# Gate one-hots laid out by token, one gate matmul a token, and the expert selection later in the weave of a 256-token network on one core

## The chip, the cores and the metric

The kernel runs on one core of a Trainium2 chip. The metric is device time of one execution in microseconds (us). "DVE" is VectorE, "ACT" ScalarE, "PE" TensorE (its weight loads are "PEld"), "POOL" GpSimd and "SP" the engine that issues the weight DMAs. Every engine runs its own list of instructions in order.

## What is computed

One layer of four token mixers, a gated feed-forward, two attentions, and at the end product-key experts; 256 tokens, model width 1024. Only the experts matter here:

```
scores of 8 heads against two sets of 128 keys   -> the 16 best of each set, with their places
sums of pairs of those                           -> the 16 best pairs, softmax over the 16: gates
expert (i, j), i and j in 0..127 (16384 of them): act = gelu(x . eu[i, j]),  out += gate * act * ev[i, j]
```

The kernel computes all 16384 experts for all 256 tokens densely, and a matrix of gates `G[i, j, t]` (nearly all zero) multiplies the activations. `G` comes from one-hot products: for a token t with its 128 chosen triples (i, j, gate), held on the 128 partitions, `G[:, :, t] = onehot(i)^T . (onehot(j) * gate)`. The one-hots are f16; so that the gate keeps its precision it is scaled by 4096 and split into a high and a low f16 part, whose two products are summed.

## The kernel before

Weights stream in units of [128, 1024] f32 (512 KB): a DMA on SP into `raw`, a copy on ACT into `hi` (`prefetch`, recorded as L139), a subtraction `lo = raw - hi` (L157) on POOL or DVE, three buffers of each. A column tile of a product is one unit and 24 matmuls of 256 columns in `dense_n` (L301): 16 with `hi`, 8 with `lo`. For the units of `eu` the subtraction is POOL's, for those of `ev` DVE's.

The experts run in two halves of 64 (j = 0..63, then 64..127). I call the parts stage A (`experts_u` of the first half: 64 units, with the selection and the first half's gates woven in), the first `experts_v`, stage B (`experts_u` of the second half with its gates woven in) and the second `experts_v`. The selection and the gates are generators; `weave(main, side, counts)` lets `main` emit a unit and then takes `counts[i]` steps of `side`. The order in which the code runs is the order of the instructions on every engine.

- `gen_a` (stage A): 8 steps of top-16 of pairs, a step of ranks, a step of softmax (an exponential on ACT between DVE work), four steps that look up the places (`ixr` by ACT, `eq` twice and a sum into `sel` by DVE), two steps that transpose `sel` on PE and make `IT`, `JT`, `GHL`; then `open_gates` (an iota on POOL) and 33 steps of `gates3`. `CA` is its list of counts.
- `gen_b` (stage B): 33 steps of `gates3`; `CB` is its list.
- A step of `gates3` makes the one-hots of 8 tokens on DVE (`oi`, `eqj`, `jg`; two buffers each) and then issues the matmuls of the 8 tokens before them (L1739 and L1740, one with the high and one with the low gate part), and the copy of the result from PSUM into `Gt` (ACT, scaled by 1/4096). `prep(0)` ends each generator; it multiplies activations by gates and splits them for the second matmul.

PSUM banks have tags: `m` four banks (held by the output sums from stage A on), `n` two, `d` two. In stages A and B of the kernel before, units and gate steps took banks of `d` and `n` in rotation.

Of the kernel before, what the change touches and what calls it, by code (L numbers as in the profile page):

```python
# [10 lines left out]
F16 = mybir.dt.float16  # L11
I32 = mybir.dt.int32
U32 = mybir.dt.uint32
AF = mybir.ActivationFunctionType
# [10 lines left out]
# ---------------------------------------------------------------- constants of the shapes alone  # L25
# [53 lines left out]
# per-partition parameters: name -> columns  # L79
# [19 lines left out]
CA = [1, 1, 0] * 8 + [1] * 36  # L99
CB = [0] * 4 + [1, 1, 0] * 18  # L100
# [11 lines left out]
def _emit(ctx, tc, I, out):  # L112
# [8 lines left out]
    BANKS = {"m": 4, "n": 2, "d": 2}  # L121
    turn_ = {"i": 0, "d": ["d"]}

    def bank(tag="m"):
        if tag == "d":
            turn_["i"] += 1
            tag = turn_["d"][turn_["i"] % len(turn_["d"])]
        return ps.tile([128, 512], F32, tag=tag, name="b" + tag, bufs=BANKS[tag])

# [11 lines left out]
    # ------------------------------------------------------------ weights: a stream of [128,1024] units  # L141
# [43 lines left out]
    # ------------------------------------------------------------ loads  # L185
# [29 lines left out]
    def rsqrt(pool, src, n, name, scale=1.0, out=None, w=None):  # L215
        """(src * scale + eps) ** -0.5 for src [128, n]."""
# [12 lines left out]
    def gained(gain, hi, lo, acc=None):  # L229
        """xT += acc; hi, lo <- the parts of xT * gain."""  # L230
# [10 lines left out]
    def stats(pool, tag="nsq", w=256, bufs=4):  # L241
        """R <- rsqrt(mean(xT^2) + eps) of a token on all partitions, Rc with tokens on partitions."""
# [51 lines left out]
    def dense_n(name, idx, o, M=128, X=None, part=None):  # L294
        """o [M,256] <- one column tile (K = 1024) of a product with X."""
# [9 lines left out]
    def dense_2(name, idx, d, X=None, part=0, of=4):  # L305
        """a part of two column tiles of a product with X, into d [128,512]: the products with X's low parts last."""
# [15 lines left out]
    def rows_into(acc, name, ks, xs, first, last, part=None):  # L322
        """acc (4 banks, 8 column tiles of 256 tokens) += some row tiles of a product, each with its parts of xs."""
# [17 lines left out]
    def columns_into(acc, name, u, xs, first, last, part):  # L341
        """acc (2 banks, 4 column tiles of 256 tokens) += two row tiles of a product, with their parts xs."""
# [12 lines left out]
    def tokens(name, u, nk, n, banks, part=None):  # L355
        """banks [tokens, n] += the product of nk row tiles with one unit, tokens on partitions."""
# [17 lines left out]
    def follow(gens, turns):  # L374
        """the generators' steps in the order of turns, what is left of them in rotation."""
# [49 lines left out]
    # ============================================================ block 1: the four mixers  # L425
# [53 lines left out]
    # ---- projections  # L479
# [135 lines left out]
    # ---- gated delta net: decays and beta, tokens on partitions  # L615
    G4 = []

    def gdn_gates():
# [35 lines left out]
        # e^G of a token in its chunk, e^(Glast - G), e^Glast  # L654
# [15 lines left out]
    # ---- gated delta net  # L670
    def gdn():
# [14 lines left out]
        # k, v with tokens on partitions  # L686
# [20 lines left out]
        # q e^G, channels on partitions  # L707
# [8 lines left out]
        # decays of pairs inside a chunk (rows (chunk parity, token), columns (tile, head, token))  # L716
# [38 lines left out]
        # inverse of the unit lower triangles, blocks doubling  # L755
# [31 lines left out]
        # w and u, then q_in - a w and a u  # L787
# [20 lines left out]
        def tok(z, e, c):  # L808
            """[64 rows, tile, pair, 64] of a [128, pair, 256] tile, for a head parity's columns."""
# [13 lines left out]
        # the state between chunks  # L823
# [70 lines left out]
    def logsig(dst, x, n, name):  # L894
        """dst <- log sigmoid(x), both in SBUF."""
# [9 lines left out]
    def pv(o, pt0, pt1, v):  # L905
        """o [64, 256] <- the transposed output of a head; v(tile) -> [128 tokens, 64]."""
# [3 lines left out]
    # ---- attention of heads that share a bank of outputs: two steps for a head  # L910
# [55 lines left out]
    def halves(z, lv):  # L966
        """[.., 256] -> [.., groups, 2, lv]"""
# [199 lines left out]
    # ============================================================ block 1: gated feed-forward with a convolution  # L1167
# [4 lines left out]
    # rotary tables from the positions  # L1172
# [92 lines left out]
    # ============================================================ block 2: two attentions  # L1265
# [66 lines left out]
    # latent attention: projections  # L1332
    def latent(n, gain, name):
        """after the job's matmuls: its scaled rows and the sums of their squares."""
# [201 lines left out]
    def act(j):  # L1536
        """the activations of the experts j and j + 1 of a half."""
# [7 lines left out]
    # ============================================================ block 2: product-key experts  # L1545
    IT = big.tile([128, 256], F16)
    JT = big.tile([128, 256], F16)
    GHL = big.tile([128, 2, 256], F16)
# [159 lines left out]
    box = {}  # L1708
# [256 lines left out]
```

## Time and profile before

| | us |
|---|---|
| time, median of three runs | 1680.62 (1679.57 to 1684.98) |
| profiled execution, span from the first to the last instruction | 1677.0 |
| what lies between that span and the median | 3.6 |
| stage A, 807.35 to 1075.02 of the profile | 267.7 |
| stage B, 1249.11 to 1494.32 | 245.2 |

The profiled execution has no time of its own but its span. A page of the profile gives the busy time of each engine; tables of stretches split it by stage; the chain of work is followed back from the last instruction, at each step to what released it; a timeline lists single instructions with start, duration and, in brackets, how long the engine stood idle ahead of it and who ended that.

### The profile page before, as it was taken

How to read it: one execution, taken by the hardware profiler on the slowest of the kernel's cores; microseconds unless marked ns; L12 is line 12 of the kernel's file. 1: busy time of each engine (PE TensorE's matmuls, PEld its weight loads, DVE VectorE, ACT ScalarE, POOL GpSimd, SP SyncE). 2: the span in 40 equal slices, each digit the busy share in tenths (PEclk: the TensorE clock that was granted, in tenths of full speed). 3: DMA queues.
4: the chain of work that ended last, by engine and by line, in shares of the span. 5: the costliest groups of instructions: out<-in, count | busy, mean ns of one | idle time of the engine just before them, and what ended most of it. 6: DMA issues, size and time to landing. Idle time of an engine off the chain costs nothing.

```text
span 1677.0 us, 27178 instructions
## 1 busy us (share of the span) xinstructions
PE 1549.2 (92%) x11060; PEld 1416.3 (84%) x11060; DVE 1017.6 (61%) x1666; ACT 763.3 (46%) x1050; POOL 736.3 (44%) x313
## 2 busy tenths in 40 slices
PE   6799898888877999989987999999999999999997
PEld 6688677788876878879987999988889999998886
DVE  5657757888886457766995333366672222236665
ACT  5633344444443444445462444544444444554444
POOL 3543135667765445685774554300036556540000
PEclk9899878999998999999998999999999999999999
DMA  5332013444443333463543333566664444466664
GB/s 209 104 97 77 28 53 117 138 151 151 151 139 114 101 92 110 144 189 114 169 144 97 103 113 113 165 196 193 194 193 135 133 126 126 127 201 199 190 191 135
DMA packets 63791, 231.41 MB, mean 138 GB/s; under 512 B 7073, under 2 KB 7602, under 8 KB 63282
## 3 DMA queue, kind: packets, MB, share of 16 engines
q1 hardware_dynamic: 62640, 226.00, 44.0%
q10 hardware_dynamic: 1026, 3.68, 0.6%
q8 instruction: 86, 1.41, 0.4%
q14 instruction: 39, 0.32, 0.1%
HBM read 228.60 MB, written 1.05 MB: 137 GB/s over the span
## 4 chain that ended last, share of the span: by engine, by line
PE 49%; DVE 2%; ACT 0%; POOL 0%; issue 0%; DVEq 0%; ACTq 0%
PE bd L301 10%; PE bn L301 10%; PE bm L1783 7%; PE bm L1785 7%; PE bm L1784 7%; PE bn L1739 2%; PE bd L1739 2%; PE bn L1740 2%; PE bd L1740 2%; DVE eq L1680 1%; DVE eq L1678 0%; DVE eq L1676 0%; DVE sel L1681 0%; DVE oi L1725 0%; ACT fy L139 0%; DVE fz L1818 0%
## 5 line engine op out<-in xcount | busy, mean ns | idle before, releaser
L157 POOL TENSOR_TENSOR lo<-raw,hi 128x1024 fp32r<-128x1024 f32 x296 | 728.4, 2475 | 745.2 <-ACT hi L139 737.4
L139 ACT ACTIVATE hi<-raw 128x1024 fp32r<-128x1024 f32 x426 | 446.2, 1056 | 187.9 <-PE bm L1784 51.8
L301 PE MATMUL bd<-Xh,hi 128*128 128x256 f32 x1096 | 287.8, 298 | 23.7 <-ACT hi L139 15.0
L301 PE MATMUL bd<-Xl,hi 128*128 128x256 f32 x1096 | 277.4, 289 | 0.7 <-DVE Xl L238 0.7
L301 PEld LDWEIGHTS bd<-Xh,hi 128*128 128x128 f32 x1096 | 216.3, 197 | 32.0 <-ACT hi L139 17.3
L301 PEld LDWEIGHTS bd<-Xl,hi 128*128 128x128 f32 x1096 | 215.9, 197 | 1.8 <-DVE Xl L238 1.0
L157 DVE TENSOR_TENSOR lo<-raw,hi 128x1024 fp32r<-128x1024 f32 x130 | 159.2, 1226 | 95.1 <-ACT hi L139 95.1
L1783 PE MATMUL bm<-hi,eh 128*128 128x512 f32 x512 | 199.2, 389 | 0.0
L1784 PE MATMUL bm<-hi,el 128*128 128x512 f32 x512 | 199.2, 389 | 0.0
L1785 PE MATMUL bm<-lo,eh 128*128 128x512 f32 x512 | 199.2, 389 | 0.0
L1725 DVE TENSOR_TENSOR oi<-iorep,IT 128x1024 f16<-128x1024 f16 x64 | 47.2, 737 | 243.7 <-PE bn L1740 128.8
L301 PE MATMUL bn<-Xh,hi 128*128 128x256 f32 x656 | 164.2, 289 | 13.0 <-ACT hi L139 13.0
L1223 DVE SCALAR_TENSOR_TENSOR fy<-fxp,prm,fy 128x256 f32<-128x256 f32 x88 | 154.0, 1769 | 15.8 <-ACT fy L139 14.2
L301 PE MATMUL bn<-Xl,hi 128*128 128x256 f32 x656 | 160.3, 283 | 0.0
L301 PE MATMUL bd<-Xh,lo 128*128 128x256 f32 x1096 | 155.3, 285 | 2.7 <-POOL lo L157 2.6
L301 PEld LDWEIGHTS bd<-Xh,lo 128*128 128x128 f32 x1096 | 142.0, 192 | 4.5 <-POOL lo L157 4.5
L301 PEld LDWEIGHTS bn<-Xh,hi 128*128 128x128 f32 x656 | 125.4, 191 | 14.8 <-ACT hi L139 14.8
L301 PEld LDWEIGHTS bn<-Xl,hi 128*128 128x128 f32 x656 | 125.0, 191 | 0.0
L1785 PEld LDWEIGHTS bm<-lo,eh 128*128 128x128 f32 x512 | 96.1, 188 | 20.1
L1783 PEld LDWEIGHTS bm<-hi,eh 128*128 128x128 f32 x512 | 96.1, 188 | 19.8
L1784 PEld LDWEIGHTS bm<-hi,el 128*128 128x128 f32 x512 | 96.1, 188 | 19.8
L301 PE MATMUL bn<-Xh,lo 128*128 128x256 f32 x656 | 92.6, 284 | 2.6 <-POOL lo L157 2.6
(583 smaller groups left out, 2640.5 us busy)
## 6 DMA issues: line engine op xcount, KB each, us to landing
raw<-in_eu SPq DMA_DIRECT2D x128, 512.0 KB, 3.6
raw<-in_ev SPq DMA_DIRECT2D x128, 512.0 KB, 4.0
raw<-in_w_in SPq DMA_DIRECT2D x61, 512.0 KB, 3.6
raw<-in_w_up SPq DMA_DIRECT2D x44, 512.0 KB, 3.6
raw<-in_w_down SPq DMA_DIRECT2D x22, 512.0 KB, 3.6
raw<-in_w_out SPq DMA_DIRECT2D x16, 512.0 KB, 3.6
raw<-in_w_query SPq DMA_DIRECT2D x16, 512.0 KB, 3.7
raw<-in_w_ba SPq DMA_DIRECT2D x4, 512.0 KB, 3.5
```

The costliest lines, as they stand in the source:

```text
L139: S.activation(o, i, f, **kw)
L157: (V if by == "v" else G).tensor_tensor(lo[:, :width], raw[:, :width], hi[:, :width].bitcast(F32), op=OP.subtract)
L301: PE.matmul(o, w[:, k * 128:k * 128 + M], x[:, k], start=n == 0, stop=n == 23)
L1223: V.scalar_tensor_tensor(y[:, i], xp[:, i, s:s + 256], P("fcw", n * 3 + s), y[:, i], op0=OP.mult, op1=OP.add)
L1680: V.tensor_add(eq[:, :, 0:w], eq[:, :, 0:w], eq[:, :, w:2 * w])
L1725: V.tensor_tensor(oi, rep, IT[:, None, ts].to_broadcast([128, 128, 8]), op=OP.is_equal)
L1739: PE.matmul(pv_[:, t, :nj], oi[:, :, t], jg[:, 0, :nj, t], start=True, stop=False)
L1740: PE.matmul(pv_[:, t, :nj], oi[:, :, t], jg[:, 1, :nj, t], start=False, stop=True)
L1783: PE.matmul(o, eh[:, i, ts], v[0][:, n_], start=False, stop=False, skip_group_check=True)
L1784: PE.matmul(o, el[:, i, ts], v[0][:, n_], start=False, stop=False, skip_group_check=True)
L1785: PE.matmul(o, eh[:, i, ts], v[1][:, n_], start=False, stop=last and j + i == nj - 1, skip_group_check=True)
```

## The change

Four things change, all from stage A on.

1. One-hots lie token by token (`[8 tokens, 64 pairs, 2]`) and not with the 8 tokens innermost. `IT`, `JT`, `GHL` hold each value twice, so that every operand's innermost run is a pair of f16. The single multiplication into `jg` becomes two, one for each gate part.
2. One matmul of 128 columns a token streams both gate parts (8 matmuls a step and not 16), four tokens to a bank, two banks a step.
3. The two parts are summed as the result is taken out of PSUM, by `tensor_reduce` on DVE (two a step) and not a copy on ACT; the 1/4096 moves into `prep`. In the selection's lookup, four adds become one `tensor_reduce`. The transposes and gate matmuls take banks of `n`, the units those of `d`.
4. `CA` and `CB` are new. In stage A the selection's first step comes after the 15th unit of 64 and not after the first, its lookups after the 29th, 31st, 33rd and 35th, its transposes after the 37th and 38th, and the gate steps from the 39th unit on, five for four units, up to the end of the stage. In stage B there is one gate step for two units up to the 57th unit, and one after each of the last six.

```diff
-CA = [1, 1, 0] * 8 + [1] * 36
-CB = [0] * 4 + [1, 1, 0] * 18
+CA = [0] * 14 + [1] * 8 + [0, 0, 1, 0] + [1, 0] * 5 + [1, 1] + [1, 1, 2, 1] * 7
+CB = [0] * 2 + [1, 0] * 28 + [1] * 6
...
-                for w in (8, 4, 2):
-                    V.tensor_add(eq[:, :, 0:w], eq[:, :, 0:w], eq[:, :, w:2 * w])
-                V.tensor_add(sel[:, i, t].rearrange("p (h k) -> p h k", h=8), eq[:, :, 0], eq[:, :, 1])
+                V.tensor_reduce(out=sel[:, i, t].rearrange("p (h k) -> p h k", h=8),
+                                in_=eq.rearrange("p h a k -> p h k a"), op=OP.add, axis=AX.X)
...
+        def pairs(z, n):
+            return z[:, :, None, :].to_broadcast([128, 8, n, 2])
+        def along(n, j=0):
+            return row[:, None, j:j + 2 * n].to_broadcast([128, 8, 2 * n]).rearrange("p t (j e) -> p t j e", e=2)
...
-            V.tensor_tensor(oi, rep, IT[:, None, ts].to_broadcast([128, 128, 8]), op=OP.is_equal)
-            V.tensor_tensor(eq[:, :nj], rep[:, j0:j0 + nj], JT[:, None, ts].to_broadcast([128, nj, 8]), op=OP.is_equal)
-            V.tensor_tensor(jg[:, :, :nj], eq[:, None, :nj].to_broadcast([128, 2, nj, 8]),
-                            GHL[:, :, None, ts].to_broadcast([128, 2, nj, 8]), op=OP.mult)
+            V.tensor_tensor(oi, along(64), pairs(IT[:, ts], 64), op=OP.is_equal)
+            V.tensor_tensor(eq, along(nj // 2, j0), pairs(JT[:, ts], nj // 2), op=OP.is_equal)
+            for i in range(2):
+                V.tensor_tensor(jg[:, :, i], eq, pairs(GHL[:, i, ts], nj // 2), op=OP.mult)
...
-                for t in range(8):
-                    PE.matmul(pv_[:, t, :nj], oi[:, :, t], jg[:, 0, :nj, t], start=True, stop=False)
-                    PE.matmul(pv_[:, t, :nj], oi[:, :, t], jg[:, 1, :nj, t], start=False, stop=True)
-                A(Gt[:, :nj, ts].rearrange("p j t -> p t j"), pv_[:, :, :nj], AF.Copy, scale=1.0 / 4096)
+                for t4 in (0, 4):
+                    p = bank("g").rearrange("p (t i j) -> p t i j", t=4, i=2)
+                    for t in range(4):
+                        PE.matmul(p[:, t, :, :nj], oi[:, t4 + t].rearrange("p a b -> p (a b)"),
+                                  jg[:, t4 + t].rearrange("p i a b -> p (i a b)"), start=True, stop=True)
+                    V.tensor_reduce(out=Gt[:, :nj, ts.start + t4:ts.start + t4 + 4].rearrange("p j t -> p t j"),
+                                    in_=p.rearrange("p t i j -> p t j i")[:, :, :nj], op=OP.add, axis=AX.X)
...
-        V.tensor_mul(w, w, box["G"][:, j:j + 2])
+        V.scalar_tensor_tensor(w, w, 1.0 / 4096, box["G"][:, j:j + 2], op0=OP.mult, op1=OP.mult)
```

What the change does to the order is seen at three places. (The change adds two lines near the top and a few more below, so that the same code stands up to 12 lines lower: L301 is L303, L139 is L141.) First DVE's row in the middle of the gates, from the one-hots of one step to those of the next, before:

```order
L1725 TENSOR_TENSOR oi<-iorep,IT 128x1024
L1726 TENSOR_TENSOR eqj<-iorep,JT 128x512
L1727 TENSOR_TENSOR jg<-eqj,GHL 128x1024
L1725 TENSOR_TENSOR oi<-iorep,IT 128x1024
L1726 TENSOR_TENSOR eqj<-iorep,JT 128x512
```

and with the change, where the sums of a step's results stand behind the one-hots of the step after it:

```order
L1736 TENSOR_TENSOR oi<-iorow,IT 128x1024
L1737 TENSOR_TENSOR eqj<-iorow,JT 128x512
L1739 TENSOR_TENSOR jg<-eqj,GHL 128x8x64 x2
L1752 TENSOR_REDUCE Gt<-bn 128x4x64 x2
L1736 TENSOR_TENSOR oi<-iorow,IT 128x1024
```

DVE's list gained two instructions that wait for PE in each step, and one more that makes one-hots. Second, PE's row at the start of a gate step, before:

```order
L1739 LDWEIGHTS oi
L1739 MATMUL bn<-jg,oi 128x64
L1740 LDWEIGHTS oi
L1740 MATMUL bn<-jg,oi 128x64
L1739 LDWEIGHTS oi
```

and with the change (a pair for each of 8 tokens):

```order
L303 MATMUL bd<-Xh,lo 128x256 x8
L1750 LDWEIGHTS oi
L1750 MATMUL bn<-jg,oi 128x128
L1750 LDWEIGHTS oi
L1750 MATMUL bn<-jg,oi 128x128
```

A step has half the weight loads and matmuls, each matmul twice as wide. Third, ACT's row around the selection's exponential (`sel<-sel`) and lookups, among the `hi` copies of the units and the activations of pairs of units, before:

```order
L139 ACTIVATE sel<-sel 128x256
L139 ACTIVATE hi<-raw 128x1024
L137 ACT_TABLE_LOAD
L139 ACTIVATE act_7913<-bd 128x512
L139 ACTIVATE hi<-raw 128x1024
L139 ACTIVATE ixr<-kix 128x2048
L139 ACTIVATE hi<-raw 128x1024
L139 ACTIVATE act_7913<-bn 128x512
L139 ACTIVATE ixr<-kix 128x2048
L139 ACTIVATE hi<-raw 128x1024 x2
```

and with the change:

```order
L141 ACTIVATE sel<-sel 128x256
L141 ACTIVATE hi<-raw 128x1024 x2
L139 ACT_TABLE_LOAD
L141 ACTIVATE act_7885<-bd 128x512
L141 ACTIVATE ixr<-kix 128x2048
L141 ACTIVATE hi<-raw 128x1024 x2
L141 ACTIVATE act_7885<-bd 128x512
L141 ACTIVATE ixr<-kix 128x2048
L141 ACTIVATE hi<-raw 128x1024 x2
```

Two units now lie between one lookup and the next, and the exponential moved from behind the 14th unit to behind the 27th.

## Rows read from the trace of the kernel before

**Rows 1.** Page, section 1: busy us, share of the span, instructions.

```profile
PE 1549.2 (92%) x11060; PEld 1416.3 (84%) x11060; DVE 1017.6 (61%) x1666; ACT 763.3 (46%) x1050; POOL 736.3 (44%) x313
```

**Rows 2.** Stretches of stages A and B: length, then busy us by engine.

```profile
core 0: us, PE busy (x) PEld busy (x) DVE busy (x) ACT busy (x) POOL busy (x), PEclk, DMA share, GB/s
807.35:902.31 94.96, 79.99 (x633) 78.90 (x632) 85.06 (x239) 43.16 (x45) 68.28 (x27) 0.91 0.45 141
902.31:1055.14 152.83, 152.83 (x1258) 151.45 (x1258) 53.21 (x93) 68.90 (x78) 74.43 (x31) 0.99 0.34 107
1055.14:1075.02 19.88, 19.88 (x170) 19.88 (x169) 6.21 (x5) 10.19 (x12) 12.30 (x5) 1.00 0.62 189
1075.02:1249.11 174.09, 174.09 (x771) 144.14 (x770) 119.47 (x126) 84.86 (x97) 4.11 (x2) 1.00 0.62 192
1249.11:1463.08 213.97, 213.97 (x1787) 212.56 (x1786) 58.30 (x93) 95.78 (x110) 128.10 (x54) 1.00 0.44 132
1463.08:1494.32 31.24, 31.24 (x265) 31.24 (x265) 6.21 (x5) 15.40 (x18) 21.93 (x9) 1.00 0.66 204
```

**Rows 3.** Chain of work in stage A's selection: start us, us, what.

```profile
847.36 4.75 PE bn L301 x40
852.13 0.49 ACT act L139
...
853.57 1.80 ACT ixr L139
855.39 2.27 DVE eq L1678
...
889.00 0.69 PE bn L1686 x2
...
898.33 2.87 DVE oi L1725
...
902.31 0.28 PE bn L1739
```

**Rows 4.** Chain of work, units (24 matmuls each) and gate steps.

```profile
915.23 2.84 PE bn L301 x24
920.05 2.84 PE bn L301 x24
...
1268.13 5.68 PE bd L301 x48
...
1275.80 2.84 PE bd L301 x24
```

**Rows 5.** Timeline of PE, first and last of one gate step's 16 matmuls.

```profile
908.25 0.32 PE L1739 MATMUL bn<-jg,oi 128*128 128x64 f16 x1
...
910.10 0.30 PE L1740 MATMUL bn<-jg,oi 128*128 128x64 f16 x1
```

**Rows 6.** Timelines of POOL and DVE at the start of stage B.

```profile
1247.40 13.07 POOL L157 TENSOR_TENSOR lo<-raw,hi 128x1024 fp32r<-128x1024 f32 x5 [0.27 <-ACT hi L139]
1260.75 2.40 POOL L157 TENSOR_TENSOR lo<-raw,hi 128x1024 fp32r<-128x1024 f32 x1 [0.29 <-ACT hi L139]
1263.59 2.39 POOL L157 TENSOR_TENSOR lo<-raw,hi 128x1024 fp32r<-128x1024 f32 x1 [0.44 <-ACT hi L139]
...
1249.15 1.34 DVE L1725 TENSOR_TENSOR oi<-iorep,IT 128x1024 f16<-128x1024 f16 x1 [1.48 <-PE bm L1785]
1250.41 2.62 DVE L1726 TENSOR_TENSOR eqj<-iorep,JT 128x512 f16<-128x512 f16 x1
1253.07 2.77 DVE L1727 TENSOR_TENSOR jg<-eqj,GHL 128x1024 f16<-128x1024 f16 x1
```

**Rows 7.** Timelines of DVE and POOL in one later gate step of stage B.

```profile
1305.62 0.69 DVE L1725 TENSOR_TENSOR oi<-iorep,IT 128x1024 f16<-128x1024 f16 x1 [3.08 <-PE bd L1740]
1306.23 0.42 DVE L1726 TENSOR_TENSOR eqj<-iorep,JT 128x512 f16<-128x512 f16 x1
1306.68 0.69 DVE L1727 TENSOR_TENSOR jg<-eqj,GHL 128x1024 f16<-128x1024 f16 x1
...
1307.67 4.75 POOL L157 TENSOR_TENSOR lo<-raw,hi 128x1024 fp32r<-128x1024 f32 x2 [2.44 <-ACT hi L139]
```

**Rows 8.** Single lines: duration ns min/median/max, first and last start, forms.

```profile
L157 POOL TENSOR_TENSOR lo<-raw,hi x296: 2343/2404/3387, 12.2 to 1486.1; 128x1024 fp32r<-128x1024 f32 x148
L157 DVE TENSOR_TENSOR lo<-raw,hi x130: 1217/1226/1227, 7.0 to 1661.2; 128x1024 fp32r<-128x1024 f32 x130
...
L1214 DVE TENSOR_TENSOR fxp<-bn,R x11: 683/684/691, 281.9 to 488.9; 128x512 f32<-128x512 f32 x11
...
L1109 DVE COPY_PREDICATED lA<-cst,bn x14: 428/436/795, 155.6 to 184.5; 128x256 f32<-128x256 uint32 x14
...
L139 ACT ACTIVATE eh<-act x64: 616/632/635, 1057.0 to 1657.7; 128x512 fp32r<-128x512 f32 x64
...
L139 ACT ACTIVATE Gt<-bn x32: 1092/1117/1133, 904.5 to 1438.1; 128x512 f32<-128x512 f32 x32
...
L1678 DVE TENSOR_TENSOR eq<-eq,ixr x4: 1225/1740/3350, 855.4 to 885.9; 128x2048 f16<-128x2048 f16 x4
```

More of the change, by code (lines that the diff above doesn't have):

```diff
@@ L121, in _emit @@
     BANKS = {"m": 4, "n": 2, "d": 2}
+    AS = {"g": "n"}
     turn_ = {"i": 0, "d": ["d"]}
@@ L127, in bank @@
             tag = turn_["d"][turn_["i"] % len(turn_["d"])]
+        tag = AS.get(tag, tag)
         return ps.tile([128, 512], F32, tag=tag, name="b" + tag, bufs=BANKS[tag])
@@ L1543, in _emit @@
     gained("fn", *XQ, out2)
-    IT = big.tile([128, 256], F16)
-    JT = big.tile([128, 256], F16)
-    GHL = big.tile([128, 2, 256], F16)
+    IT = big.tile([128, 256, 2], F16)
+    JT = big.tile([128, 256, 2], F16)
+    GHL = big.tile([128, 2, 256, 2], F16)
     tk = ExitStack()
@@ L1678, in second @@
                 V.tensor_mul(eq, eq, ixr)
-                for w in (8, 4, 2):
-                    V.tensor_add(eq[:, :, 0:w], eq[:, :, 0:w], eq[:, :, w:2 * w])
-                V.tensor_add(sel[:, i, t].rearrange("p (h k) -> p h k", h=8), eq[:, :, 0], eq[:, :, 1])
+                V.tensor_reduce(out=sel[:, i, t].rearrange("p (h k) -> p h k", h=8),
+                                in_=eq.rearrange("p h a k -> p h k a"), op=OP.add, axis=AX.X)
                 yield
         for t in range(2):
-            p = bank("d")
+            p = bank("g")
             for i in range(3):
@@ L1687, in second @@
             ts = slice(t * 128, t * 128 + 128)
-            V.tensor_copy(IT[:, ts], p[:, 0:128])
-            V.tensor_copy(JT[:, ts], p[:, 128:256])
+            two = lambda z: z[:, :, None].to_broadcast([128, 128, 2])
+            V.tensor_copy(IT[:, ts], two(p[:, 0:128]))
+            V.tensor_copy(JT[:, ts], two(p[:, 128:256]))
             gs = ktmp.tile([128, 128], F32, tag="gs", name="gs", bufs=1)
             V.tensor_scalar(gs, p[:, 256:384], 4096.0, None, op0=OP.mult)
-            V.tensor_copy(GHL[:, 0, ts], gs)
-            V.tensor_sub(GHL[:, 1, ts], gs, GHL[:, 0, ts])
+            V.tensor_copy(GHL[:, 0, ts], two(gs))
+            V.tensor_sub(GHL[:, 1, ts], two(gs), GHL[:, 0, ts])
             yield
     def experts_u(j0, nj):
+        turn_["d"] = ["d"]
         d = None
@@ L1713, in open_gates @@
         box["w"] = wx.enter_context(tc.tile_pool(name="wtmp", bufs=2))
-        box["r"] = box["w"].tile([128, 128, 8], F16, name="iorep", bufs=1)
-        G.iota(box["r"], pattern=[[1, 128], [0, 8]], base=0, channel_multiplier=0, allow_small_or_imprecise_dtypes=True)
+        box["r"] = box["w"].tile([128, 128], F16, name="iorow", bufs=1)
+        G.iota(box["r"], pattern=[[1, 128]], base=0, channel_multiplier=0, allow_small_or_imprecise_dtypes=True)
     def gates3(j0, nj):
-        Gt, wtmp, rep = box["G"], box["w"], box["r"]
-        def one_hots(ts):
-            oi = wtmp.tile([128, 128, 8], F16, tag="w1", name="oi")
-            jg = wtmp.tile([128, 2, 64, 8], F16, tag="w2", name="jg")
-            eq = wtmp.tile([128, 64, 8], F16, tag="w3", name="eqj")
-            V.tensor_tensor(oi, rep, IT[:, None, ts].to_broadcast([128, 128, 8]), op=OP.is_equal)
-            V.tensor_tensor(eq[:, :nj], rep[:, j0:j0 + nj], JT[:, None, ts].to_broadcast([128, nj, 8]), op=OP.is_equal)
-            V.tensor_tensor(jg[:, :, :nj], eq[:, None, :nj].to_broadcast([128, 2, nj, 8]),
-                            GHL[:, :, None, ts].to_broadcast([128, 2, nj, 8]), op=OP.mult)
+        Gt, wtmp, row = box["G"], box["w"], box["r"]
+        def pairs(z, n):
+            return z[:, :, None, :].to_broadcast([128, 8, n, 2])
+        def along(n, j=0):
+            return row[:, None, j:j + 2 * n].to_broadcast([128, 8, 2 * n]).rearrange("p t (j e) -> p t j e", e=2)
+        def one_hots(ts):
+            oi = wtmp.tile([128, 8, 64, 2], F16, tag="w1", name="oi")
+            jg = wtmp.tile([128, 8, 2, nj // 2, 2], F16, tag="w2", name="jg")
+            eq = wtmp.tile([128, 8, nj // 2, 2], F16, tag="w3", name="eqj")
+            V.tensor_tensor(oi, along(64), pairs(IT[:, ts], 64), op=OP.is_equal)
+            V.tensor_tensor(eq, along(nj // 2, j0), pairs(JT[:, ts], nj // 2), op=OP.is_equal)
+            for i in range(2):
+                V.tensor_tensor(jg[:, :, i], eq, pairs(GHL[:, i, ts], nj // 2), op=OP.mult)
             return ts, oi, jg
```

2 lines of the change are left out of this document (removed).

## The prediction

> **What bounds the kernel now.** I read the busy times first, then the stretches of stages A and B, then the chain of work through them, then single rows of DVE and POOL. PE is busy for 92% of the span and no other engine for more than 61% [rows 1]. The change lies in stages A and B alone, apart from one multiplication in `prep`. In both, a unit takes PE 2.84 us, and a gate step pushes the next unit back by 920.05 - 915.23 - 2.84 = 1.98 us in A and 1275.80 - 1268.13 - 5.68 = 1.99 us in B [rows 4]. So 64 units are 181.8 us and 32 gate steps 63.4 us. Stage B lasts 213.97 + 31.24 = 245.2 us [rows 2], which is exactly this sum: PE never waits there. Stage A lasts 94.96 + 152.83 + 19.88 = 267.7 us; 22.5 us are left over. The chain shows where: from 852.13 to 902.31 it goes through ACT's `ixr`, DVE's `eq` and the first `oi` and only now and then through PE [rows 3]. The selection's DVE work is not ready when PE comes to it, and since ACT's `ixr` stand in the same list as the units' `hi`, the units stop too.
>
> **A limit that the busy shares hide.** POOL's `lo` takes 2.40 us (median) at whatever time [rows 8]. At the start of stage B POOL has five of them in a row (13.07 us), and DVE's one-hots of that time took 1.34, 2.62 and 2.77 us [rows 6]; in a step with POOL idle the same three took 0.69, 0.42 and 0.69 [rows 7]. The excess of the last two, 2.20 and 2.08, is nearly one `lo` each. So a DVE instruction with both inputs in SBUF and a `lo` exclude each other, and when both queues are full they take turns. A DVE instruction with one input in PSUM doesn't: `fxp<-bn,R` took 683 to 691 ns in all eleven cases, in a stage full of `lo`s [rows 8]. The Trainium skill (SBUF — State Buffer, "Who interferes with whom") says the same of instructions with two SBUF inputs and adds that `tensor_reduce` never contends on this chip; no run here shows that for a `tensor_reduce`. If it did contend, both stages would go to the upper ends worked out below and the time to 1717.
>
> **PE's part of the change.** A step had 16 matmuls, (910.10 - 908.25) / 15 = 0.123 us apart [rows 5]. It now has 8 of 128 columns. If the pace stays, a step costs 0.98 us; if the matmul's columns set it, as in a unit (2.84 / 24 = 0.118 us for 256 columns [rows 4]), it is 0.059 us each, 0.47 us a step. I take 0.6, nearer the lower end, since both operands are now read in one run. That frees 64 x 1.38 = 88 us of PE.
>
> **DVE's part.** `oi` and `eqj` keep their sizes (0.69 and 0.42 us [rows 7]). `jg` becomes two instructions of 512 elements, 0.42 each by `eqj`. One-hots: 1.95 us a step, from 1.80. New are two `tensor_reduce` over 512 PSUM elements each. No row has one. The lower end is a 128x512 instruction out of PSUM, 0.69 us [rows 8]. The upper comes from two rows of short strided runs: ACT's copy into `Gt`, which writes at the same stride as the reduce will, takes 1117 ns where a 128x512 copy in one run takes 632, and the masked copy L1109 goes from 436 to 795 ns [rows 8], 1.8 times either way: 1.2 us. I take 0.69, since the reduce writes only one element for two that it reads. DVE's work for a step is then 1.95 + 1.38 = 3.33 us. ACT loses 64 copies of 1.1 us, worth nothing: it is busy for about half of both stages or less [rows 2]. `prep` keeps one instruction of the same size; in the `experts_v` stage between A and B DVE is busy for 119.5 of 174.1 us while PE never stops [rows 2], so I cost it at nothing.
>
> **Stage B.** Two units and one step: PE needs 5.68 + 0.6 = 6.28 us, but `lo`s and one-hots, which exclude each other, need 2 x 2.40 + 1.95 = 6.75. (Before, three units and two steps: 7.2 + 3.6 = 10.8 of PE's 12.5.) So POOL and DVE together become the bound. For the stage that is 64 x 2.40 + 32 x 1.95 = 216 us, and 3 us at the end (the last reduces, `prep`'s multiplication and `eh` at 0.63 lie between the last gate matmuls and the next stage): 219 us if all reduces fall beside a `lo`; if none does, 32 x 1.38 = 44 us more, 263. Each `lo` starts soon after a unit's end (one every 2.84 us [rows 6]), which is also when a gate step's matmuls end, so most reduces should be covered. I take a fifth of the way: 228 us, 17 less than before.
>
> **Stage A.** The first 38 units have no gate step: 107.9 us. The selection's top-16 work on DVE waits for no unit, so it runs as early as before; the lookups now follow ACT's `ixr` after the 29th unit, 807.35 + 29 x 2.84 = 889.7. A lookup is two f16 instructions of 1.23 us (the least of L1678 [rows 8]) and a `tensor_reduce` over 2048 elements: twice the 1.226 us of a 1024-element instruction [rows 8], so 2.4, or 4.4 at the strided price. With up to one `lo` ahead of each of the first two, a lookup is between 4.9 and 11.7 us; I take 7. Four end at 917.7, where PE reaches the second transposes at 807.35 + 38 x 2.84 = 915.3: about 2 us of stall in place of 22. With 2 us for the first one-hots and 3 at the end, 7 us. The other 26 units carry 32 steps, five for four units: PE needs 11.36 + 3.0 = 14.4 us for four units, but `lo`s and one-hots 9.6 + 9.75 = 19.4, and with the reduces uncovered 26.3. Times 6.5: 126 to 171 us. Stage A is 241 to 286 us. Here I go six tenths of the way, because the order works against cover: the reduces of a step stand behind the next step's one-hots in DVE's list (every `lo` that gets between holds them up), PE's next gate matmuls wait for the two `n` banks that these reduces empty, and where two steps follow one unit there is no `lo` to cover them. 268 us: no gain.
>
> **Sum.** Stage A 0, stage B -17. The profiled span is 1677.0 and the median 1680.6, so 3.6 us lie around the span and stay. Forecast 1680.6 - 17 = 1664 us, 1% faster, though PE loses 88 us of work and the selection's stall. About 0.3% (5 us) is what a measurement of this kernel can tell from no change.
>
> **Rivals.** (1) *All reduces covered*: A 241, B 219, 53 us less, 1628. For it: DVE is idle between steps in B today (3.08 us ahead of the `oi` in [rows 7]); against it: the order in A. (2) *PE stays the bound*: 181.8 + 19.2 a stage with 7 and 3 us at the edges, 208 and 204, 101 us less, 1580. Only if one-hots and `lo`s overlapped, against [rows 6]. (3) *The reduce at its strided price, 1.2 us* (the other side): DVE needs 4.35 us a step. Its list alone then takes 5 x 4.35 = 21.8 us for four units of A, 141 + 115 = 256 us for the stage; serial with the `lo`s 31.4, 319 us. Longer reduces cover more of the `lo`s, so four tenths of the way: 281, 13 more than before. B: 219 to 219 + 32 x 2.4 = 296; a quarter of the way is 238, 7 less. 1687, slower by 6. Between 0.69 (-17) and 1.2 (+6) the sign turns at about 1.1 us. The Trainium skill (SBUF — State Buffer, "Door 1") says that accesses which change lines of 16 bytes in SBUF, or 8 in PSUM, are penalised; the reduce's two parts lie 256 bytes apart. The 1117 ns of the `Gt` copy agree for the write. (4) *One-hots lose their double rate*: with pairs as the innermost run `oi` would go at the 1.23 us of a 1024-element f32 instruction [rows 8] and the 512-element ones at 0.69, 3.3 us a step. Then even with full cover B is 154 + 106 + 3 = 263 and A 6.5 x 26.1 + 115 = 285: 35 us more, 1716 or above. Today's runs of 8 elements go at the double rate. The Trainium skill (VectorE: DVE Perf Modes, "What auto-detection actually checks") asks only for 16-bit tensors with a step of one, which pairs keep; by it this doesn't happen, and no row here has runs of two f16.
>
> **Chances and range.** Forecast (1645 to 1677) 0.50, rival 1 0.14, rival 2 0.05, rival 3 0.23, rival 4 0.08. Faster by over 0.3%: the forecast but for 0.05 of it at the range's slow end, rivals 1 and 2, and 0.02 of rival 3 (a reduce below 1 us): 0.66. Slower: rival 4 and 0.14 of rival 3, 0.22. The same: those 0.05 and 0.07 of rival 3, 0.12. Rival 3 reaches a little past 1687 and rival 1 a little below 1628 if the stall or the edges are smaller; leaving out rivals 2 and 4 and about half of the far end of rival 1, the range is 1628 to 1690. The forecast's own range is 1645 to 1677.
>
> **What would show it.** The gate matmuls 0.06 to 0.09 us apart; the reduces near 0.69 us; in stage A PE idle ahead of gate matmuls, waiting for DVE's one-hots or reduces, in the last 26 units; one-hot instructions of 2.5 us and more beside `lo`s; stage B near 228 us with POOL and DVE taking turns; hardly any stall before the 38th unit. Wrong if stage A's last 26 units run at PE's 14.4 us for four, or if the reduces take over 1 us.

## The result, and the profile after

The changed kernel takes 1630.07 us (median of 4 runs, 1629.17 to 1631.03); the kernel before, on the same chip, 1680.8 (4 runs). The ratio is 0.9698, with an interval of 0.9676 to 0.9719: 3% faster, about 51 us, where 17 were forecast. The page's busy times of after, as in [rows 1]:

```profile
PE 1469.7 (90%) x10548; PEld 1333.4 (82%) x10548; DVE 1223.1 (75%) x1846; ACT 707.4 (43%) x986; POOL 745.4 (46%) x313
```

PE lost 79.5 us of work and DVE gained 205.5. The stages of after (length, then busy us by engine and the granted clock, as in [rows 2]): stage A, the `experts_v` stage behind it, stage B.

```profile
808.12:1066.75 258.63, 217.94 (x1799) 212.68 (x1798) 217.91 (x417) 94.56 (x104) 156.90 (x63) 0.92 0.43 131
1066.75:1243.36 176.61, 176.61 (x770) 145.77 (x771) 120.80 (x129) 84.36 (x96) 4.12 (x2) 0.99 0.62 186
1243.36:1445.45 202.09, 199.30 (x1794) 196.95 (x1793) 194.90 (x193) 84.10 (x98) 157.39 (x63) 1.00 0.56 172
```

Counted from the first matmul of the first unit (807.59 in before), the stages took 267.4, 174.1 and 245.2 us before. So A gave 8.8 us and B 43.1; `experts_v` took 2.5 more and all else 0.6 more, together 48.8 less, the difference of the spans (1677.0 and 1628.2); the other 1.9 us lie outside the profiled spans. The 2.5 us go with PE's clock: A now ends with PE waiting (2.2 us ahead of the first matmul of `experts_v`), and the next stage starts at the lower of the clock's two levels (1.2 and 2.4 GHz): the granted clock is 0.51 of full speed in the first 4.5 us and 1.00 behind them. In the chain of work its first matmuls stand 0.43 us apart, later ones 0.23. (Chains are shown here without pieces of a few hundredths of a us that are called "issue".)

```profile
1068.27 0.43 PE bm L1797
1068.69 0.43 PE bm L1795
```

The new operations, as single lines (ns least, median, greatest): reductions of the gates, gate matmuls and their weight loads, and the lookup's reductions.

```profile
L1752 DVE TENSOR_REDUCE Gt<-bn x128: 674/681/695, 935.4 to 1441.6; 128x256 f32<-128x512 f32 x128
...
L1750 PEld LDWEIGHTS <-oi x512: 95/98/151, 931.6 to 1440.5; 128*128 128x128 f16 x171
L1750 PE MATMUL bn<-jg,oi x512: 216/219/314, 931.6 to 1440.6; 128*128 128x128 f16 x171
...
L1681 DVE TENSOR_REDUCE sel<-eq x4: 3832/4376/4410, 892.9 to 920.0; 128x128 f32<-128x2048 f16 x4
```

All 128 gate reductions take the lower price of 0.68 us, `lo` or no `lo` (by the timelines a `lo` runs beside 39% of their time in A and 89% in B), and although the two numbers that they add lie 256 bytes apart in PSUM. The Trainium skill (SBUF — State Buffer, "Who interferes with whom") says that `tensor_reduce` never contends on this chip: these rows agree. What the Trainium skill says of lines of 8 bytes in PSUM (same page, "Door 1") names matmuls; read as a rule for these reductions too, it would have made them dearer, and these rows show no such penalty. The lookup's reductions, out of SBUF, have four times the elements of a gate reduction and take 5.6 to 6.5 times as long: they cost what the forecast had put as the strided price, 4.4 us. No run varies their stride.

**Stage B.** One period of the chain (two units and a step), and POOL and DVE in another period's timeline:

```profile
1259.12 1.66 DVE oi L1736
1260.78 0.34 DVE eqj L1737
...
1261.15 2.97 DVE jg L1739 x2
1264.12 1.20 DVE Gt L1752 x2
1265.32 1.65 DVE oi L1736
```

```profile
1316.89 2.97 DVE L1739 TENSOR_TENSOR jg<-eqj,GHL 128x512 f16<-128x512 f16 x2
1316.92 2.65 POOL L159 TENSOR_TENSOR lo<-raw,hi 128x1024 fp32r<-128x1024 f32 x1 [0.95 <-ACT hi L141]
...
1319.33 0.62 PE L1750 MATMUL bn<-jg,oi 128*128 128x128 f16 x8
...
1319.76 2.40 POOL L159 TENSOR_TENSOR lo<-raw,hi 128x1024 fp32r<-128x1024 f32 x1 [0.19 <-PE bn L1750]
1319.78 1.28 DVE L1752 TENSOR_REDUCE Gt<-bn 128x256 f32<-128x512 f32 x2
```

A period is 1265.32 - 1259.12 = 6.20 us; 32 of them are 198. POOL and DVE do take turns: one `lo` falls between the two `jg` (2.97 us in place of 0.76), the other over the reductions and the start of `oi`. But in turns they need less than forecast, as the rows in A say in which no `lo` is in the way.

**Stage A.** The chain at the selection's first and last lookup, and pieces of it from the last 26 units:

```profile
889.76 1.80 ACT ixr L141
...
916.80 3.19 DVE eq L1680
...
920.02 3.84 DVE sel L1681
...
923.91 0.69 PE bn L1687 x2
...
938.29 0.35 DVE eqj L1737
...
938.66 0.76 DVE jg L1739 x2
...
962.55 0.58 PE bn L1750 x4
963.13 3.94 PE bd L303 x24
967.07 0.25 PE bn L1750 x4
...
967.35 1.29 DVE Gt L1752 x2
968.64 1.66 DVE oi L1736
...
970.67 2.97 DVE jg L1739 x2
973.63 1.20 DVE Gt L1752 x2
...
1005.96 0.58 PE bn L1750 x4
...
1061.13 0.60 DVE oi L1736
```

PE stood still for 7.4 us ahead of the transposes at 923.91. From 935 us to the end of the stage the chain lies on DVE for 71% and on PE for 27%, and DVE is busy for 116.5 of the 122 us from 940 to 1062. Four units and five steps take (1005.96 - 962.55) / 2 = 21.7 us, where PE has work for 4 x 2.84 + 5 x 0.50 = 13.9. Behind the longest waits PE runs at its lower level for a while: granted clock 0.69 from 962.55 to 967.07, behind a wait of 3.46 us, and 1.00 in the 3 us after. Four gate matmuls take 0.58 us there and 0.25 later, and the unit between them 3.94 where it needs 2.84 [rows 4]. Who waits for whom at this place:

```profile
961.95 1.18 PE L1750 MATMUL bn<-jg,oi 128*128 128x128 f16 x8 [3.46 <-DVE Gt L1752]
...
967.35 2.40 POOL L159 TENSOR_TENSOR lo<-raw,hi 128x1024 fp32r<-128x1024 f32 x1 [7.74 <-PE bn L1750]
```

PE waits for DVE's reductions, because a gate step now takes both banks of `n` and finds them full; POOL waits for PE.

**What an instruction really holds.** Where one DVE instruction follows another at once, the chain gives the distance from start to start: 0.60 for `oi`, 0.35 for `eqj`, 0.76 for the two `jg`: 1.71 a step, not the 1.95 that durations add up to; 0.60 for a reduction, not 0.69. And a `lo` lengthens the pair of `jg` by 2.97 - 0.76 = 2.2 us, not 2.40. A duration ends with a tail in which the next instruction already runs.

### The profile page after: what moved, and what is told of

Read it like the earlier page. It is cut to its first block, busy times and chain, and to the rows that moved or that the text cites. A ratio compares the mean times of both kernels' runs of the same rounds, so it can differ in the third digit from the quotient of the medians.

```text
span 1628.2 us, 26256 instructions
## 1 busy us (share of the span) xinstructions
PE 1469.7 (90%) x10548; PEld 1333.4 (82%) x10548; DVE 1223.1 (75%) x1846; ACT 707.4 (43%) x986; POOL 745.4 (46%) x313
## 5 line engine op out<-in xcount | busy, mean ns | idle before, releaser
L141 ACT ACTIVATE hi<-raw 128x1024 fp32r<-128x1024 f32 x426 | 445.7, 1054 | 393.7 <-PE bd L303 235.0
L303 PE MATMUL bd<-Xh,hi 128*128 128x256 f32 (+1 forms) x1592 | 416.3, 297 | 21.9 <-ACT hi L141 13.4
L303 PE MATMUL bd<-Xl,hi 128*128 128x256 f32 (+1 forms) x1592 | 403.7, 289 | 0.7 <-DVE Xl L240 0.7
L303 PEld LDWEIGHTS bd<-Xh,hi 128*128 128x128 f32 (+1 forms) x1592 | 314.5, 198 | 29.8 <-ACT hi L141 15.5
L303 PEld LDWEIGHTS bd<-Xl,hi 128*128 128x128 f32 (+1 forms) x1592 | 314.4, 198 | 1.9 <-DVE Xl L240 1.0
L303 PE MATMUL bd<-Xh,lo 128*128 128x256 f32 (+1 forms) x1592 | 224.8, 284 | 2.9 <-POOL lo L159 2.8
L303 PEld LDWEIGHTS bd<-Xh,lo 128*128 128x128 f32 (+1 forms) x1592 | 206.1, 192 | 4.9 <-POOL lo L159 4.9
L1739 DVE TENSOR_TENSOR jg<-eqj,GHL 128x512 f16<-128x512 f16 x128 | 127.9, 1040 | 2.2
L1736 DVE TENSOR_TENSOR oi<-iorow,IT 128x1024 f16<-128x1024 f16 x64 | 98.8, 1544 | 2.4 <-PE bm L1797 2.0
L141 ACT ACTIVATE eh<-act 128x512 fp32r<-128x512 f32 x64 | 40.4, 632 | 127.0 <-DVE act L1778 127.0
L1752 DVE TENSOR_REDUCE Gt<-bn 128x256 f32<-128x512 f32 x128 | 81.9, 682 | 9.9 <-PE bn L1750 9.8
L1750 PE MATMUL bn<-jg,oi 128*128 128x128 f16 x512 | 45.1, 227 | 32.6 <-DVE Gt L1752 32.5
```

Of the source, the lines that this page charges most:

```text
L141: S.activation(o, i, f, **kw)
L303: PE.matmul(o, w[:, k * 128:k * 128 + M], x[:, k], start=n == 0, stop=n == 23)
L1736: V.tensor_tensor(oi, along(64), pairs(IT[:, ts], 64), op=OP.is_equal)
L1739: V.tensor_tensor(jg[:, :, i], eq, pairs(GHL[:, i, ts], nj // 2), op=OP.mult)
L1750: PE.matmul(p[:, t, :, :nj], oi[:, t4 + t].rearrange("p a b -> p (a b)"), jg[:, t4 + t].rearrange("p i a b -> p (i a b)"), start=True, sto ...
L1752: V.tensor_reduce(out=Gt[:, :nj, ts.start + t4:ts.start + t4 + 4].rearrange("p j t -> p t j"), in_=p.rearrange("p t i j -> p t j i")[:, :, ...
```

## The experiments

**Theory:** with these times stage B needs 2 x 2.2 + 1.71 = 6.1 us of POOL and DVE in turns, and its reductions lie beside a `lo`, so PE still bounds it; stage A is bound by DVE, and there the new reductions cost. **Rivals:** stage B is bound by the turns; the reductions are covered in A too; the new order by itself gives the gain. Stage lengths below are taken from each run's chain as above. Ratios are to the kernel before on the same chip (1679.2 to 1681.5 us there).

| run | median us | ratio (interval) | A | B |
|---|---|---|---|---|
| before | 1680.8 | 1 | 267.4 | 245.2 |
| changed | 1630.07 | 0.9698 (0.9676 to 0.9719) | 258.6 | 202.1 |
| order_alone | 1685.28 | 1.0035 (1.0024 to 1.0046) | 267.1 | 247.7 |
| old_order | 1637.79 | 0.9752 (0.9735 to 0.9768) | 251.2 | 220.2 |
| adds | 1632.35 | 0.9718 (0.97 to 0.9735) | 263.6 | 202.1 |
| no_lo | 1590.09 | 0.9454 (0.9421 to 0.9487) | 218.9 | 199.6 |
| act_sum | 1607.01 | 0.9548 (0.9518 to 0.9578) | 236.2 | 202.0 |
| dve_lo | 1612.99 | 0.96 (0.9579 to 0.962) | 244.3 | 202.1 |
| early_sel | 1609.62 | 0.9572 (0.955 to 0.9594) | 242.5 | 202.1 |
| reduces_first | 1667.27 | 0.9919 (0.9898 to 0.994) | 288.8 | 210.4 |
| act_early | 1593.24 | 0.9494 (0.9478 to 0.951) | 222.6 | 202.0 |
| act_early_dve | 1575.25 | 0.9377 (0.9364 to 0.9389) | 206.5 | 202.0 |
| strided_oi | 1633.51 | 0.9727 (0.9713 to 0.9742) | 260.5 | 204.9 |
| strided_jg | 1676.34 | 0.998 (0.9971 to 0.9989) | 267.8 | 241.1 |
| pack_only | 1605.49 | 0.9556 (0.9515 to 0.9597) | 236.4 | 205.2 |

**order_alone**: the kernel before, with

```diff
-CA = [1, 1, 0] * 8 + [1] * 36
-CB = [0] * 4 + [1, 1, 0] * 18
+CA = [0] * 14 + [1] * 8 + [0, 0, 1, 0] + [1, 0] * 5 + [1, 1] + [1, 1, 2, 1] * 7
+CB = [0] * 2 + [1, 0] * 28 + [1] * 6
```

> The kernel before with nothing but the two lists CA and CB of the change. Theory (the new lists are worth something by themselves, because the selection's work then lies under units that need nothing of it): stage B stays bound by PE at 181.8 + 63.4 = 245 us; stage A loses most of its 22.5 us of stall, its last 26 units being bound by PE at 4 x 2.84 + 5 x 1.98 = 21.3 us for four units: 248 to 256 us, the whole 1662 to 1670 us. Rival (the lists help only with the packed one-hots): stage A within 3 us of 267.7, the whole 1678 to 1685.

The theory of this run fell and its rival held: A stays at 267.1 us. The lookups now end at 926.4 us, 37 later than before, and half of their 16 additions still take 2.3 us or more beside a `lo`. The 0.35% that it is slower lie elsewhere: B is 2.5 us longer, and the `experts_v` stage between takes 177.4 us in place of 174.1, with the same slow start as in the changed kernel.

**old_order**: the reverse edit on the changed kernel.

> The changed kernel with the lists CA and CB of before. Theory: in stage B two gate steps lie in three units, so that one-hots and lo instructions that exclude each other need 3 x 2.2 + 2 x 1.72 = 10.0 us where PE needs 9.5, and part of the reduces comes on top: stage B 212 to 225 us against 201 in the changed kernel; stage A has its lookups early and stalls longer for the strided reduces, 258 to 272: the whole 1640 to 1665 us. Rival (the packing does it all, the order nothing): within 5 us of 1630.

B as expected: with two steps in three units POOL and DVE become the bound, and the order is worth 18 us there. A not, nor the whole (1637.79, below the range): the old order is 7.4 us better in A, where its lookups end 36 us earlier in the stage.

**adds**: the changed kernel with

```diff
-                V.tensor_reduce(out=sel[:, i, t].rearrange("p (h k) -> p h k", h=8),
-                                in_=eq.rearrange("p h a k -> p h k a"), op=OP.add, axis=AX.X)
+                for w in (8, 4, 2):
+                    V.tensor_add(eq[:, :, 0:w], eq[:, :, 0:w], eq[:, :, w:2 * w])
+                V.tensor_add(sel[:, i, t].rearrange("p (h k) -> p h k", h=8), eq[:, :, 0], eq[:, :, 1])
```

> The changed kernel with the selection's lookup summed by four additions as before, in place of one reduction of 4.4 us. Theory: PE's wait of 7.4 us for the second transposes comes from the four reductions; with the additions, at most 1.4 us in all if no lo is in the way and 3.6 if one is, the wait falls to between 0 and 3 us and the whole to 1622 to 1627 us. Rival (additions wait for a lo each and so take as long): within 2 us of 1630.

The rival held in kind (the time is 2.3 us longer, a little beyond its range). The chain of this run shows the first lookup's additions, each behind a `lo`, and the last one's without:

```profile
890.16 2.78 DVE eq L1682
892.97 2.51 DVE eq L1682
895.50 2.39 DVE eq L1682
897.91 2.38 DVE sel L1683
...
923.79 0.70 DVE eq L1682
924.52 0.43 DVE eq L1682
924.97 0.30 DVE eq L1682
925.30 0.30 DVE sel L1683
```

10 us or 1.7 for the same work; the reduction, 3.8 to 4.4 us in all four lookups, is no loss against that: with it A is 5 us shorter.

**no_lo**: the changed kernel, which here leaves out the low parts of 90 units' weights.

```diff
+        if name == "eu" and idx >= 38:
+            lo = hi
+        else:
...
```

> The changed kernel without the low parts of the experts_u weights from the 39th unit of stage A to the end of stage B: hi is read in place of lo, so the output is another, with as many matmuls of the same shapes. POOL is then idle there. Theory (stage B is bound by PE; the last 26 units of stage A by DVE, which stands still while a lo has the port): stage B stays at 201 us within 3 although all one-hots run at 0.35 to 0.69 us; in stage A four units with five gate steps go from 21.5 us to between DVE's own 5 x 2.92 = 14.6 and 15.5 us, 39 to 45 us less in the stage, the whole 1585 to 1592. Rival (stage B is bound by lo instructions and one-hots taking turns, and its 6.19 us for two units only happens to be near PE's 6.18): stage B would also fall where PE could go faster, by more than 5 us.

The times came out as the theory said in both stages. One period of its chain in stage B:

```profile
1295.06 5.73 PE bd L306 x48
1300.79 0.46 PE bn L1753 x8
```

5.73 + 0.46 = 6.19 us, within 0.01 the period of the changed kernel: with POOL idle and all one-hots at 0.42 to 0.69 us, B is 199.6 us, only 2.5 less. There PE is the bound, although the chain of the changed kernel goes through DVE: two loops of nearly equal length, of which the chain names one. In A 39.7 us go. But the chain there is not DVE's list, as the theory has it: it lies on PE for 82%, and once in four units on two reductions, where a second step follows the first at once and waits for the banks of `n`:

```profile
965.20 0.25 PE bn L1753 x4
965.47 1.30 DVE Gt L1755 x2
966.82 0.38 PE bn L1753 x4
```

**act_sum**: the changed kernel with

```diff
-                for t4 in (0, 4):
-                    p = bank("g").rearrange("p (t i j) -> p t i j", t=4, i=2)
...
+                p = bank("g").rearrange("p (t j) -> p t j", t=8)
+                for t in range(8):
+                    w = oi[:, t].rearrange("p a b -> p (a b)")
+                    for i in range(2):
+                        PE.matmul(p[:, t, :nj], w, jg[:, t, i].rearrange("p a b -> p (a b)"), start=i == 0, stop=i == 1)
+                A(Gt[:, :nj, ts].rearrange("p j t -> p t j"), p[:, :, :nj], AF.Copy)
```

> The changed kernel with its packed one-hots, but high and low parts as two accumulating matmuls of 64 columns per token, and ACT's copy into Gt as before in place of the two reductions. Theory (with the times for which instructions hold DVE: a lo shuts it out for 2.2 us, a step's one-hots take 1.72, its reductions 1.20 of which in stage A two thirds lie beside no lo): stage A's last 26 units go from 21.5 us for four units to the larger of 4 x 2.2 + 5 x 1.72 = 17.4 and PE's 4 x 2.84 + 5 x 1.0 = 16.4, about 25 us less, A 232 to 238; stage B is bound by PE at 64 x 2.84 + 32 x 1.0 = 214 plus the ends, 216 to 220 from 202; the whole 1618 to 1625 us. Rival (the reductions are covered in A too, what binds it is something else): A stays at 259 within 4, B as above, the whole 1643 to 1650.

A as expected: without DVE's reductions it is 22.4 us shorter. (The edit also lets a step take one bank and not two; no run parts the two effects.) B and the whole are better than expected (202.0 for 216 to 220, 1607 for 1618 to 1625), because 16 packed matmuls of 64 columns cost PE no more than 8 of 128, as the chain in B and the single lines show:

```profile
1291.18 0.48 PE bn L1751 x16
1291.66 5.75 PE bd L303 x48
```

```profile
L1751 PEld LDWEIGHTS <-oi x1024: 95/98/133, 932.6 to 1417.4; 128*128 128x128 f16 x171
```

0.48 / 16 = 0.030 us a matmul, with its own weight load of 98 ns hidden. So the wide matmul saves PE nothing, and the sum that it leaves to DVE, with the second bank, is a loss of 23 us on the whole kernel.

**dve_lo**: the changed kernel with

```diff
-        plan(*[("eu", i, 1024) for i in range(lo_, hi_)], by="g")
+        for i in range(lo_, hi_):
+            plan(("eu", i, 1024), by="v" if 38 <= i < 64 else "g")
```

> The changed kernel with the lo of the experts_u units 39 to 64 (the last 26 of stage A) on DVE in place of POOL. Theory (a lo on POOL shuts DVE out for 2.2 us, one on DVE holds it for 1.13): DVE's list for four units and five steps is 4 x 1.13 + 5 x 2.92 = 19.1 us against 21.5 now, 10 to 16 us less in the stage: A 243 to 249, the whole 1614 to 1621. Rival (POOL and DVE mostly run side by side, and DVE's own work is the bound): A longer by 26 x 1.13 less what DVE now waits, 10 to 29 us more, the whole 1640 to 1659.

The theory held in A (244.3); the whole is 1 us below its range. A `lo` that DVE makes itself costs it less (1.13 us in this run's chain) than one on POOL that shuts it out.

**early_sel**: the changed kernel with

```diff
-CA = [0] * 14 + [1] * 8 + [0, 0, 1, 0] + [1, 0] * 5 + [1, 1] + [1, 1, 2, 1] * 7
+CA = [1] * 9 + [0] * 7 + [2, 0, 1, 0, 1, 0, 1] + [0] * 5 + [1, 2] + [1] * 32
```

> The changed kernel with another CA: the exponential behind unit 17 in place of 27 and the lookups behind units 19, 21 and 23 and with the exponential, the transposes behind units 29 and 30, and then one gate step behind each of 32 units. Theory (DVE stands idle for 30 us ahead of the selection's normalisation because ACT's exponential is listed late, and stage A ends when DVE's list does): the lookups end near 891 us in place of 924, the wait of 7.4 us ahead of the transposes goes, and the gate steps take 4.46 us each as in the old order: A 236 to 246 us, the whole 1607 to 1618. Rival (stage A is bound by the sum of POOL's and DVE's work wherever the steps stand): A within 5 us of 258.6, the whole 1625 to 1635.

It held. (The list also spreads the gate steps to one a unit; no run parts that from the earlier selection.) DVE's timeline of the changed kernel has the 30 us that this order takes out:

```profile
884.42 0.42 DVE L1669 TENSOR_REDUCE smk<-sel 128x16 f32<-128x256 f32 x1 [30.36 <-ACT sel L141]
```

**reduces_first**: the changed kernel with

```diff
-            new = one_hots(slice(t0, t0 + 8)) if t0 < 256 else None
             if prev:
...
-            prev = new
+            prev = one_hots(slice(t0, t0 + 8)) if t0 < 256 else None
```

> The changed kernel with each step's two reductions ahead of the next step's one-hots in DVE's list, not behind them. Theory (reductions are covered where a lo runs at the same time, and one-hots made early keep PE from waiting; the place in the list makes no cover by itself): B stays at 202 us within 4; in A, where two steps follow one unit, the second step's matmuls now wait for reductions and one-hots in a row, so A is 259 to 280 and the whole 1630 to 1652. Rival (the reductions are uncovered in A because they stand behind the one-hots, as the prediction has it): A falls towards full cover, 17.4 us for four units, by 10 to 26 us, the whole 1604 to 1620.

Slower beyond both ranges: matmuls, reductions and one-hots now follow each other in a chain, in B too. The place of the reductions in the list was right. Nor did the other place give cover: in this run a `lo` runs beside 34% of their time in A, in the changed kernel beside 39%.

**act_early** joins act_sum and early_sel; **act_early_dve** adds dve_lo, for units 31 to 64.

> The changed kernel with both of two edits that each helped alone: ACT's copy with accumulating matmuls in place of DVE's reductions, and the list CA that brings the selection early and then one gate step behind each unit. Theory (DVE's list ends the stage; a gate step then costs 2.2 of a lo and 1.72 of one-hots, 3.9 us for a unit and a step): the gate steps run from about 895 us on and end after 32 x 3.9 = 125, stage A 214 to 224 us and the whole 1583 to 1597. Rival (the two edits take away the same wait): A not below 232, the whole 1602 or more.

> As act_early, with the lo of the experts_u units 31 to 64 of stage A on DVE in place of POOL. Theory: a unit and a step then ask 1.13 + 1.72 = 2.85 us of DVE and 2.84 + 0.5 = 3.34 of PE, so PE bounds the rest of the stage: A 198 to 208 us, the whole 1567 to 1582. Rival (what is left in act_early is a wait other than DVE's, for ACT's hi or the chain of one step): A within 5 us of act_early.

Both held. The last takes 1575.25 us where the changed kernel takes 1630.07, 55 us less. Its chain through A's gate steps is PE's alone, 2.92 + 0.48 = 3.40 us for a unit and a step:

```profile
987.31 0.48 PE bn L1752 x16
987.79 2.92 PE bd L303 x24
```

**strided_oi and strided_jg**: the changed kernel with, in the first and in the second,

```diff
-                        PE.matmul(p[:, t, :, :nj], oi[:, t4 + t].rearrange("p a b -> p (a b)"),
+                        PE.matmul(p[:, t, :, :nj], oi.rearrange("p t a b -> p (t a b)").rearrange("p (c t) -> p t c", t=8)[:, t4 + t],
...
-                                  jg[:, t4 + t].rearrange("p i a b -> p (i a b)"), start=True, stop=True)
+                                  jg.rearrange("p t i a b -> p (t i a b)").rearrange("p (c t) -> p t c", t=8)[:, t4 + t], start=True, stop=True)
```

> The changed kernel in which TensorE's weights of a gate matmul are read from oi with a step of 8 elements, as before the change (columns of several tokens are mixed, so the gates are others); one-hots and all else as changed. Theory W (before, the weight load of 146 ns with a step of 16 bytes set the 0.123 us from matmul to matmul, not the columns): a step costs PE 8 x 0.123 = 0.98 us in place of 0.50, which lengthens stage B, which PE bounds, by 15 us, and the whole to 1645 to 1655. Rival M (the strided read of the moving operand set it): nothing changes, 1630 within 4.

> The changed kernel in which the moving operand of a gate matmul is read from jg with a step of 8 elements, as before the change (tokens are mixed, so the gates are others). Theory W (the weight load set the pace before): nothing changes, 1630 within 4. Rival M (the strided read of the moving operand set it, 64 columns in 0.123 us and so 128 in up to 0.25): a step costs 1.0 to 2.0 us in place of 0.50, stage B 15 to 48 us more, the whole 1645 to 1700.

Rival M held in both. The chain in B of strided_oi, and then of strided_jg:

```profile
1301.27 0.56 PE bn L1750 x8
1301.82 5.73 PE bd L303 x48
```

```profile
1303.05 1.82 PE bn L1750 x8
1304.87 5.68 PE bd L303 x48
```

A weight load at a step of 16 bytes takes 148 ns (median) in place of 98, but costs PE only 0.1 us a step. The moving operand at that step costs 1.82 / 8 = 0.228 us for 128 columns, four times the packed price and close to twice the 0.123 of 64 columns before [rows 5].

**pack_only**: the changed kernel with the edits of act_sum, adds and old_order together, so the kernel before with the packed one-hots, and with the changed kernel's banks for units and gates and its 1/4096 in `prep`.

> The kernel before with the packed one-hots alone: two accumulating matmuls of 64 columns per token and ACT's copy, the lookup's four additions and the lists CA and CB stay as before. Theory (the packed moving operand gives the whole gain; the wide matmul, the reductions on DVE and the new order are each worth nothing or less, except the order in stage B): stage B is bound by lo and one-hots at 3 x 2.2 + 2 x 1.72 = 10.0 us for three units and two steps, 200 to 212 us; stage A keeps its stall at the selection and then needs 3.9 us for a unit with a step, 232 to 248; the whole 1598 to 1622 us, less than the changed kernel's 1630. Rival (reductions and order carry part of the gain): the whole 1632 or more.

It held: the packing gives 76 us (68 to 82 by the interval), more than the whole change. What the banks do in it was not run by itself; in B before, where PE never waits [rows 2], they had nothing to give. The packing of the moving operand alone is worth 46 us inside the changed kernel (strided_jg).

## Why the prediction was right in sign and wrong in size

**The bound before, and PE's part: right.** PE bounded both stages but for the stall at the selection, and a gate step went from 1.98 us to 6.19 - 5.68 = 0.51 in a period of no_lo (forecast 0.6, bounds 0.47 and 0.98). The reason is what the forecast left open: strided_jg, and act_sum's 0.030 us for 64 packed columns, show that the moving operand's step had set the 0.123 us.

**The price of taking turns: the step that failed.** The forecast put a `lo` at 2.40 us and a step's one-hots at 1.95, durations both, so "`lo`s and one-hots, which exclude each other, need 2 x 2.40 + 1.95 = 6.75", more than PE's 6.28. Held times give 2 x 2.2 + 1.71 = 6.1, less than PE's measured 6.19. So the bound of stage B did not move to POOL and DVE; rival 2's outcome (PE stays the bound, 204) holds in that stage, though not by the overlap that it asked for: `lo`s and one-hots do take turns, only at a lower price. The two prices are 32 x (6.75 - 6.19) = 18 us of the 26 by which B was missed (228 forecast, 202 measured). The rows for it were there: in [rows 7] `oi` and `eqj` start 0.61 us apart, and the forecast itself read 2.20 and 2.08 us of excess out of [rows 6]. Another reading was weaker than told: of the eleven `fxp<-bn,R` only the first, at 281.9 us, lay beside a `lo`; the others started as a `lo` ended. That an instruction out of PSUM isn't held up rests on the 128 reductions now.

**Reductions in stage B: mis-sized.** "A fifth of the way" was 9 us for uncovered reductions. A ninth of their time lies beside no `lo`, so the cover was guessed well enough; but act_sum, which has no reductions, leaves B at 202.0: where PE is the bound they cost nothing.

**Stage A: two errors against each other.** By held times four units and five steps lie between 4 x 2.2 + 5 x 1.71 = 17.4 us and 23.4 (with 5 x 1.20 of reductions); measured were 21.7, about seven tenths of the way where six were taken (by the timelines 61% of the reductions' time lies beside no `lo`). So the cover was well guessed and the ends of that range were too dear: 6.5 x (19.4 + 0.6 x 6.9 - 21.7) = 12 us too much. The reason given, that the reductions stand behind the next one-hots, is not borne out: reduces_first puts them ahead and covers no more. In the other direction the stall ahead of the transposes was 7.4 us, not 2. The step behind it is "A lookup ... I take 7": the four took 923.87 - 889.76 = 34.1 us with ACT's first `ixr`, 8.5 each, with the reduction at the upper of its two prices. A was forecast at 268 and is 258.6 from its first unit on; the two errors make 7 of these 9 us, the rest is not accounted for. Of the signs that the forecast named, matmuls 0.06 us apart, reductions near 0.69 us, one-hots of 2.5 us and more (`oi` up to 2.89) and PE waiting for DVE in the last 26 units came true; B near 228 us and "hardly any stall before the 38th unit" did not.

**What was not in the sum.** The selection's DVE work "runs as early as before", but only to the exponential, which the new list puts 35 us later (849.3 us before, 884.0 now); early_sel gains 16 us in A with a list that undoes this. And the 2.5 us at the start of `experts_v`, where PE has waited and the granted clock is 0.51.

**The rivals.** Rival 1 (1628) gave the nearest time, by luck: it asks for full cover in both stages, A had none such, and B a different bound. Rival 2 fell in A (208 forecast, 258.6). Rival 3 fell: 0.68 us in all 128 reductions. Rival 4 fell: `eqj` and `jg` have medians of 413 and 425 ns, the double rate.

What stays open: why in A six tenths of the reductions' time lie beside no `lo`. That POOL there waits for PE, and PE for the banks that DVE's reductions empty, is seen in the timeline; no run varies it alone. That fewer instructions that take turns help is shown (no_lo, act_sum, dve_lo).

## What to carry to other kernels

Price an instruction of a full queue by the distance from its start to the next one's, and an exclusion by the excess that it causes, not by durations: a bound that stands 7% over another can be an error of adding tails. Look for strided moving operands of small matmuls first; packing them was worth 76 us here, without the wide matmul, the reductions and the new order. Before a sum moves from PE's accumulation to an engine that already takes turns with another, ask what PE saves by it: here nothing, and it cost 23 us with the second bank that it took.

## What the hardware showed that was not expected

- A 16-bit moving operand read at a step of 16 bytes costs PE 0.228 us for 128 columns, packed 0.058 (0.46 / 8); the same step in the weights adds about 0.01 us a matmul.
- Two packed accumulating matmuls of 64 columns, each with its weight load, cost as much as one of 128 (0.48 and 0.46 us a step).
- A slow reduction (4.4 us) is no worse than four fast additions (1.7 us alone) where each of them waits for another engine's turn (10 us).
